# A hybrid decoder layer on one core: background work is offered a turn at each pair of main products instead of every six, with other constants in its estimate of time

## The chip, the cores and the metric

The kernel runs on one core of one Trainium2 chip. Its time is the device time of one execution in microseconds (us), given as the median of three runs. The engines of a core are named as in the profile: PE is TensorE's matrix products, PEld its weight loads, DVE is VectorE, ACT is ScalarE, POOL is GpSimd, SP is SyncE, which issues most DMAs here.

## The reference

One step of a decoder layer for two groups of requests that share all weights: a prompt of 512 new tokens, and eight sequences with one new token each. Width is 2048, everything is float32.

```
mod = silu(c) @ w_ada + b_ada              # 2048 x 12288, split into six parts
h = modulate(rmsnorm(x), sh1, sc1)
q, k, v, p_rwkv = split(h @ w_in)          # 4896 columns
att = sliding-window attention(q, k, v)    # 16 heads of 64, window 128, ALiBi, sinks
rw, S = RWKV-7 mixing(p_rwkv, S0)          # 16 heads of 64, a state recurrence over tokens
x = x + gt1 * (concat(att, rw) @ w_out)
h2 = modulate(rmsnorm(x), sh2, sc2)
x = x + gt2 * ((silu(gate) * up) @ w_ffn_out),   gate, up = split(h2 @ w_ffn_in)
y = rmsnorm(x)
```

Results are y for both groups, the new key and value windows, the new recurrent states and the last projection rows.

## The kernel before

**Main products.** Activations are kept transposed, 128 features by 2 x 260 columns (256 prompt tokens and four of the eight single tokens in each half). For precision each weight tile and each activation is split into a high and a low part of a reduced float32 type: `unit` (L81) loads 128 x 512 weights, ACT copies the high part (L88), DVE subtracts to get the low part (L91). `mm3` (L94) then issues three pairs of products for one block of 128 x 128 weights: high weights with the high activations, high with low, low with high, and in each pair one product for each half of the columns. These are the main products, `pm` in the profile for the input projection and the feed-forward part, `po` for the output projection, `pf` for the last projection. `main_tile` (L103) makes one tile of 128 output features from 16 blocks.

**Background work.** All that isn't such a product is written as generators, called jobs: the conditioning vectors (`ada_part` L272 in the startup, `ada_gen` L295 later, 256 steps of four small float32 products, each after a load of 256 KB), the RWKV mixing in eight pairs of heads (`rwkv_prep1`, `rwkv_prep2` and `rwkv_rest`, L530 to L790: preparation, a triangular solve in 31 steps on DVE, then a chain of 16 chunks with two steps each, where PE makes four records named `psc<-Z,L` or `psc<-Z,LS` and DVE and ACT copy them back), the attention in eight pairs of heads (`attn_pair` L857), the eight single tokens (`rwkv_sample` L1030, `attn_decode` L932), loads and splits (`cat_load` L1241), and the second norm (`norm_half` L1204). A job gives up its turn by `yield`.

**Who runs when.** `pump` (L123) is one turn. It advances the planner's clock of PE by the time that the main products since the last turn are thought to take, and then goes through the jobs: one that is due runs to its next `yield`, and its instructions come at this place of the program. When a job is next due is worked out by `spent` (L113): each instruction that a job issues through the `Paced` engines (L32 to L61) books a time on its engine's clock (a fixed part and a part per element) and moves `done_at`; what `done_at` is at the `yield` is when the job is due again. `main_tile`, `part_tile`, `wout_part` call `pump` once for each block, that is after six products, and `wout_half` (L1283) after three. A job that wants to wait yields more than once, or adds to `done_at`. `drain` (L137) and waiting loops call `pump` without main products.

The program order made in this way is not the last word: when the program is built, each engine's instructions are put in a list by a scheduler that prefers the earlier instruction and passes one whose inputs it doesn't think ready.

**Order of the kernel.** Startup (norm of x, the first two parts of the conditioning in stages, five first tiles); the RWKV phase with 39 tiles of the input projection in all, of which 12 are fillers (`filler` L437) that are taken when the next tile would have to wait for a buffer; the attention phase, whose main products are the output projection; the second norm, half by half, beside the last quarter of the output projection; and then the feed-forward part (`ffn_phase` L1307), in which no job is alive.

Of the kernel before, what the change touches and what calls it, by code (L numbers as in the profile page):

```python
# [8 lines left out]
F32R = mybir.dt.float32r  # L9
# [5 lines left out]
P = 128  # L15
# [16 lines left out]
class Paced:  # L32
# [5 lines left out]
    def __getattr__(self, name):  # L38
        f = getattr(self.eng, name)

        def call(out, *a, **kw):
            if name == "dma_start":
                self.kern.spent(self.eng, 1.0, 1.5)
            else:
                per = self.per
                if name == "matmul" and a[0].dtype == F32R:
                    per /= 4
                self.kern.spent(self.eng, self.base + per * math.prod(out.shape[1:]), 0.1)
            return f(out, *a, **kw)  # L49
        return call  # L50


class PacedCore:
    def __init__(self, kern):
        nc = kern.nc
        self.nc = nc
        self.tensor = Paced(kern, nc.tensor, 0.0017, 0.06)
        self.vector = Paced(kern, nc.vector, 0.0011, 0.08)
        self.scalar = Paced(kern, nc.scalar, 0.001, 0.2)
        self.gpsimd = Paced(kern, nc.gpsimd, 0.0023, 0.1)  # L60
        self.sync = Paced(kern, nc.sync, 0, 0)  # L61


class Kern:
    def __init__(self, tc, I, O, upto="all"):
        self.tc, self.nc, self.I, self.O, self.upto = tc, tc.nc, I, O, upto
        self.n = 0
        self.bg = []
        self.free, self.done_at = {}, 0.0
        self.px = PacedCore(self)  # L70
        self.nada = 0
        self.sample_done = self.kv_done = self.decode_done = False
        self.cat_out, self.cat_in = set(), 0
        self.psc = None
        self.squares = [None, None]
# [15 lines left out]
        nc.vector.tensor_tensor(wl[:, :n], raw[:, :n], wh[:, :n].bitcast(F32), ALU.subtract)  # L91
        return wh, wl

    def mm3(self, ps, m, wh, wl, aH, aL, k, first, last, halves=((0, 0), (1, 1))):  # L94
        nc = self.nc
        for i, (w, a) in enumerate(((wh, aH), (wh, aL), (wl, aH))):
            for h, bank in halves:
                nc.tensor.matmul(  # L98
                    ps[:m, bank, :HB], w, a[:, k, h, :],
                    start=first and i == 0, stop=last and i == 2, skip_group_check=True,  # L100
                )

    def main_tile(self, dram, aH, aL, ncol=128):  # L103
        ps = self.ps_m.tile([P, 2, 512], F32, tag="m", name=self.nm("pm"))
        for k in range(KD):
            if k % 4 == 0:
                wh, wl = self.unit(dram[:, k * ncol:(k + 4) * ncol])
            s = slice(k % 4 * ncol, (k % 4 + 1) * ncol)
            self.mm3(ps, ncol, wh[:, s], wl[:, s], aH, aL, k, k == 0, k == KD - 1)
            self.pump()  # L110
        return ps

    def spent(self, eng, us, more=0.0):  # L113
# [6 lines left out]
        self.free[self.nc.tensor] = self.free.get(self.nc.tensor, 0.0) + us  # L120
        return self.free[self.nc.tensor]

    def pump(self, us=0.62):  # L123

        self.now(us)
        for job in list(self.bg):
            if job[1] > self.now():
                continue
            self.done_at = self.now()
            if next(job[0], "end") == "end":  # L130
                self.bg.remove(job)
            job[1] = self.done_at

    def start(self, gen):
        self.bg.append([gen, 0.0])
# [136 lines left out]
    def ada_part(self, f):  # L272

        nc = self.nc
        ps = self.aux_c(f // 2 % 2)
        for kg in range(4):
            tag, n = (("RR", 2), ("L3", 3), ("As", 1), ("L3", 3), ("RR", 2), ("L3", 3))[self.nada % 6]
            self.nada += 1
            raw = self.rc.tile([P, 1024], F32, tag=tag, bufs=n, name=self.nm("araw"))
            nc.sync.dma_start(raw, self.I["w_ada1"][f // 2, kg])  # L280
            self.ada_mm(ps, raw, kg, 0, 256)
            self.spent(nc.tensor, 0.45)
            self.done_at += 0.7
            yield
        yield from self.ada_finish(f, 2, ps)
# [9 lines left out]
    def ada_gen(self):  # L295
        nc = self.px
        for c in (GT1, SH2, SC2, GT2):
            for q in range(4):
                ci = c // 4 + q
                ps = self.hold("ada")  # L300
                for k in range(KD):
                    raw = self.w.tile([P, 512], F32, tag="ar", bufs=3, name=self.nm("ar"))
                    nc.sync.dma_start(raw, self.I["w_ada2"][ci - 8, k])
                    for j in range(4):
                        self.nc.tensor.matmul(
                            ps[32 * j:32 * j + 32, 0:128], self.cT[:, k, :], raw[:, j * 128:(j + 1) * 128],
                            start=k == 0, stop=k == KD - 1, tile_position=(0, 32 * j), skip_group_check=True,
                        )
                    self.spent(self.nc.tensor, 0.3)
                    yield  # L310
                    yield
                res = self.w.tile([P, 512], F32, tag="ar", bufs=3, name=self.nm("adar"))[:, 0:128]
                nc.scalar.copy(res, ps[:, 0:128])
                yield
                p2 = self.aux("adT")
                nc.tensor.transpose(p2[:, 0:128], res, self.ident)
                nc.vector.tensor_tensor(
                    self.mod[:, 4 * ci:4 * ci + 4, :], p2[:, 0:128].rearrange("p (f t) -> p f t", f=4)[:, :, 0:9],
                    self.par[:, P_BA + 4 * ci:P_BA + 4 * ci + 4].unsqueeze(2).broadcast_to([P, 4, 9]), ALU.add)
# [86 lines left out]
    def part_tile(self, src, m, out, sout, k0, k1):  # L406
        nc = self.nc
        wh, wl = self.unit(src[:, k0 * m:k1 * m])
        ps = self.ps_m.tile([P, 2, 512], F32, tag="m", name=self.nm("pm"))
        for k in range(k0, k1):  # L410
            s = slice((k - k0) * m, (k - k0 + 1) * m)
            self.mm3(ps, m, wh[:, s], wl[:, s], self.hH, self.hL, k, k == k0, k == k1 - 1)
            self.pump()
        out = out.rearrange("p (h t) -> p h t", h=2)
        ps = ps[:m]
        sps = ps[:, :, HB - sout.shape[-1]:HB]
        if k0 == 0:
            nc.scalar.copy(out, ps[:, :, 0:256])
            nc.scalar.copy(sout, sps)
        else:  # L420
            nc.vector.tensor_tensor(out, out, ps[:, :, 0:256], ALU.add)
            nc.vector.tensor_tensor(sout, sout, sps, ALU.add)
# [107 lines left out]
    def rwkv_prep1(self, d):  # L530
# [13 lines left out]
        sq = t512("tF")  # L544
        k = self.shift_mix(8 + hp, sq)
        nc.scalar.activation(sq, k, AF.Square, scale=col(P_KK))
        for _ in range(3):
            yield
        pw = self.aux("pw")
        for i in range(2):  # L550
            nc.tensor.matmul(pw, lw[i][:, 0:128], self.LW, start=i == 0, stop=i == 1)
# [121 lines left out]
    def rwkv_rest(self, d):  # L673
# [103 lines left out]
        wh, wl = self.lora(hp, 384)  # L777
        nc.scalar.copy(wh[64:128, 128:256], wl[64:128, 128:256].bitcast(F32))
        yield
        for _ in range(3):  # L780
            yield
        pg = self.aux("pg")
        for i, (w, g) in enumerate(((wh, self.SG0[0]), (wh, self.SG0[1]), (wl, self.SG0[0]))):
            nc.tensor.matmul(pg, w[:, 0:128], g, start=i == 0, stop=False)
# [483 lines left out]
    def wout_part(self, k0, k1):  # L1268
        nc, I = self.nc, self.I
        while self.cat_in < k1 or (k0 == 8 and not self.decode_done):  # L1270
            self.pump()
        n = k1 - k0
        for o in range(KD):
            ps = self.ps_m.tile([P, 2, 512], F32, tag="m", name=self.nm("po"))
            for kk in range(n):
                if kk % 4 == 0:
                    wh, wl = self.unit(I["w_out"][o, :, (k0 + kk) * 128:(k0 + kk + 4) * 128])
                s = slice(kk % 4 * 128, (kk % 4 + 1) * 128)
                self.mm3(ps, P, wh[:, s], wl[:, s], *self.cat[0], k0 + kk, kk == 0, kk == n - 1)
                self.pump()  # L1280
            self.accumulate(o, ps, GT1)

    def wout_half(self, h, kept):  # L1283
# [3 lines left out]
        for o in range(0, KD, 2):  # L1287
            mt = lambda: self.ps_m.tile([P, 2, 512], F32, tag="m", name=self.nm("po"))
            ps = mt()
            for j in range(2):  # L1290
                if o + j not in kept:
                    pool = dict(pool=self.wk, bufs=6) if o in (2, 6, 10) else {}
                    u = self.unit(self.I["w_out"][o + j, :, 12 * 128:16 * 128], **pool)
                    if pool:
                        kept[o + j] = u
                wh, wl = kept.get(o + j, u)
                for kk in range(4):
                    s = slice(kk * 128, (kk + 1) * 128)
                    self.mm3(ps, P, wh[:, s], wl[:, s], *self.cat[1], kk, kk == 0, kk == 3, ((h, j),))
                    self.pump(0.4)  # L1300
                if o == KD - 2:
                    self.accumulate_half(o + j, 1, ps[:, j:j + 1], GT1, h)
                    ps = mt()
            if o < KD - 2:
                self.accumulate_half(o, 2, ps, GT1, h)
# [233 lines left out]
```

## Time and profile before

| what | value |
|---|---|
| median of three runs | 2763.02 us (2754.31 to 2765.76) |
| the profiled execution | 2761.62 us |
| its span, first to last instruction | 2759.8 us |
| busy: PE, PEld, DVE, ACT, POOL | 97%, 90%, 49%, 33%, 8% |
| mean granted clock of PE | 0.982 |
| main products: startup and input projection / output projection / feed-forward | 3744 / 1536 / 12672 |
| idle time of PE in the span | 80 us |

A row of the order of time is: start, duration, engine, line of the kernel, operation, output tile <- inputs, shape of the array's tile, shape of the data, number of records; in brackets idle time before it and the instruction that ended it. A float32 product shows as two records, one of the reduced type as one. L49 is the line of the helper that passes on the instructions of all jobs, so these are told apart by the names of their tiles. Products are pipelined: a row's duration is longer than its distance to the next, and the time that a group costs is read from the starts. A row of the waits is: engine, what waited, what it waited for, total us, times, longest.

### The profile page before, as it was taken

The page shows a single profiled execution, that of the slowest core. Times are in us where ns is not written, and L with a number is a line of the kernel's source. Part 1 is how long each engine was busy: PE and PEld are TensorE (multiplying, and loading weights), DVE is VectorE, ACT ScalarE, POOL GpSimd, SP SyncE. Part 2 cuts the span into 40 slices and gives each one's busy share as a digit, 9 for nine tenths or more (in the row PEclk, how much of TensorE's full clock was granted, in tenths as well). Part 3 has the DMA queues.
Part 4 walks back from the last instruction along what each step waited for, and adds up shares of the span by engine and source line. Part 5 has one row for each costly group of instructions (what it writes and reads, how often), then busy time and mean ns, then how long its engine had stood idle before and what let it go on. Part 6 is the DMA issues. An engine that isn't in the chain of part 4 may idle for free.

```text
span 2759.8 us, 58911 instructions
## 1 busy us (share of the span) xinstructions
PE 2679.3 (97%) x24461; PEld 2479.0 (90%) x24461; DVE 1356.5 (49%) x3266; ACT 923.4 (33%) x1816; POOL 223.6 (8%) x300
## 2 busy tenths in 40 slices
PE   7899999999999999989999999999999999999998
PEld 5577777887787898979999999999999999999997
DVE  2465677767755465682434343434343434343436
ACT  3133445455432344552222222222222222222225
POOL 1012122222111000130000000000000000000004
PEclk9899999999989999999999999999999999999999
DMA  8865554555556732322222222222222222222223
GB/s 296 308 200 149 153 152 141 161 150 151 175 163 206 255 133 100 113 80 92 91 93 90 93 92 93 92 92 93 92 93 92 92 93 92 93 92 93 90 96 110
DMA packets 189900, 354.25 MB, mean 128 GB/s; under 512 B 27665, under 2 KB 38849, under 8 KB 189345
## 3 DMA queue, kind: packets, MB, share of 16 engines
q1 hardware_dynamic: 185584, 339.30, 37.1%
q0 software_dynamic: 3408, 10.15, 1.2%
q8 instruction: 191, 3.13, 0.5%
q10 hardware_dynamic: 640, 1.05, 0.1%
q14 instruction: 77, 0.62, 0.1%
HBM read 332.86 MB, written 18.55 MB: 127 GB/s over the span
## 4 chain that ended last, share of the span: by engine, by line
PE 59%; DVE 2%; DMA 1%; ACT 1%; POOL 0%; issue 0%; DVEq 0%; SPq 0%; ACTq 0%; POOLq 0%
PE pm L98 36%; PE pf L98 18%; PE po L98 3%; PE pl L49 1%; PE pO L49 0%; PE pt L49 0%; PE psc L49 0%; DVE wl L91 0%; DVE x L1178 0%; DMA raw<-in_w_fi 0%; DVE h2L L49 0%; DVE u L49 0%; ACT h2H L49 0%; DMA raw<-in_w_out 0%; POOL u L49 0%
## 5 line engine op out<-in xcount | busy, mean ns | idle before, releaser
L88 ACT CAST wh<-raw 128x512 fp32r<-128x512 f32 (+2 forms) x751 | 460.9, 615 | 1266.8 <-PE pm L98 807.1
L91 DVE TENSOR_TENSOR wl<-raw,wh 128x512 fp32r<-128x512 f32 (+2 forms) x751 | 522.3, 697 | 690.2 <-ACT wh L88 688.8
L98 PE MATMUL pm<-h2H,wh 128*128 128x260 f32 x2816 | 571.2, 282 | 2.2 <-ACT wh L88 1.2
L98 PE MATMUL pm<-h2L,wh 128*128 128x260 f32 x2816 | 572.1, 283 | 0.7 <-DVE h2L L49 0.4
L98 PE MATMUL pm<-h2H,wl 128*128 128x260 f32 x2816 | 572.4, 283 | 0.0
L98 PEld LDWEIGHTS pm<-h2H,wh 128*128 128x128 f32 x2816 | 435.9, 188 | 2.9 <-ACT wh L88 1.3
L98 PEld LDWEIGHTS pm<-h2L,wh 128*128 128x128 f32 x2816 | 435.0, 188 | 1.7 <-DVE h2L L49 1.5
L98 PEld LDWEIGHTS pm<-h2H,wl 128*128 128x128 f32 x2816 | 436.3, 188 | 0.0
L98 PE MATMUL pm<-hH,wh 128*128 128x260 f32 (+1 forms) x1248 | 297.6, 318 | 2.8 <-ACT hH L143 1.6
L98 PE MATMUL pf<-gH,wh 128*128 128x260 f32 x1312 | 266.8, 283 | 0.0
L98 PE MATMUL pf<-gH,wl 128*128 128x260 f32 x1312 | 266.4, 282 | 0.0
L98 PE MATMUL pf<-gL,wh 128*128 128x260 f32 x1312 | 266.4, 282 | 0.0
L98 PE MATMUL pm<-hL,wh 128*128 128x260 f32 (+1 forms) x1248 | 264.7, 292 | 0.2 <-DVE hL L144 0.2
L98 PE MATMUL pm<-hH,wl 128*128 128x260 f32 (+1 forms) x1248 | 262.5, 291 | 0.0
L98 PEld LDWEIGHTS pm<-hH,wh 128*128 128x128 f32 (+1 forms) x1248 | 195.9, 192 | 51.8 <-issue 33.1
L1167 DVE SCALAR_TENSOR_TENSOR x<-pf,mod,x 128x512 f32<-128x512 f32 x160 | 120.1, 750 | 215.1 <-PE pf L98 215.1
L98 PEld LDWEIGHTS pf<-gH,wl 128*128 128x128 f32 x1312 | 203.4, 188 | 0.0
L98 PEld LDWEIGHTS pf<-gL,wh 128*128 128x128 f32 x1312 | 203.2, 188 | 0.0
L98 PEld LDWEIGHTS pf<-gH,wh 128*128 128x128 f32 x1312 | 203.2, 188 | 0.0
L98 PEld LDWEIGHTS pm<-hH,wl 128*128 128x128 f32 (+1 forms) x1248 | 197.6, 192 | 6.0 <-issue 1.8
L98 PEld LDWEIGHTS pm<-hL,wh 128*128 128x128 f32 (+1 forms) x1248 | 198.0, 192 | 5.4 <-issue 2.0
L1186 POOL TENSOR_TENSOR acc<-sqh 128x260 f32<-128x260 f32 x4 | 3.0, 742 | 1662.1 <-ACT sqh L1183 1471.3
(372 smaller groups left out, 3100.2 us busy)
## 6 DMA issues: line engine op xcount, KB each, us to landing
raw<-in_w_fi SPq DMA_DIRECT2D x352, 256.0 KB, 2.5
ar<-in_w_ada SPq DMA_DIRECT2D x256, 256.0 KB, 3.1
raw<-in_w_fo SPq DMA_DIRECT2D x176, 256.0 KB, 2.5
raw<-in_w_in SPq DMA_DIRECT2D x148, 256.0 KB, 3.6
araw<-in_w_ada SPq DMA_DIRECT2D x64, 512.0 KB, 6.0
raw<-in_w_out SPq DMA_DIRECT2D x74, 256.0 KB, 2.9
catl<-catd SPq DMA_DIRECT2D x16, 256.0 KB, 2.8
x<-in_x SPq DMA_DIRECT2D x4, 780.0 KB, 7.8
```

Of the source, the lines that this page charges most:

```text
L49: return f(out, *a, **kw)
L88: nc.scalar.copy(wh[:, :n], raw[:, :n])
L91: nc.vector.tensor_tensor(wl[:, :n], raw[:, :n], wh[:, :n].bitcast(F32), ALU.subtract)
L98: nc.tensor.matmul(ps[:m, bank, :HB], w, a[:, k, h, :], start=first and i == 0, stop=last and i == 2, skip_group_check=True,)
L1167: nc.vector.scalar_tensor_tensor(x[:, :, 0:256], ps[:, :, 0:256], self.mod[:, gt + o, 0:1], x[:, :, 0:256], ALU.mult, ALU.add)
L1186: nc.gpsimd.tensor_tensor(acc, sq[:, 0], sq[:, 1], ALU.add)
```

## The change

`mm3` gets an argument `pump` and offers a turn after each pair of products; `main_tile`, `part_tile` and `wout_part` use it and no longer pump once for six. The time that a turn adds to the planner's clock goes from 0.62 for six products to 0.243 for two. The estimate of an instruction's time changes for PE: another slope and fixed part, 0.12 for a transpose, 0.05 for a product on a part of the array, a quarter for the reduced type as before. A turn in which a job used PE now adds 0.2 (`switched`). Jobs that waited by yielding several times now yield once and add a time to `done_at`: 1.6 for each step of `ada_gen`, 2.2 in `rwkv_prep1` and `rwkv_rest`. Turns without main products add 0.73 in place of 0.62, and the half-product loop 0.37 in place of 0.4. No instruction is added or removed.

```diff
@@ Paced.call
-                per = self.per
-                if name == "matmul" and a[0].dtype == F32R:
-                    per /= 4
-                self.kern.spent(self.eng, self.base + per * math.prod(out.shape[1:]), 0.1)
+                us = self.base + self.per * math.prod(out.shape[1:])
+                if name == "transpose":
+                    us = 0.12
+                elif name == "matmul":
+                    us = 0.05 if kw.get("tile_position") else us / 4 if a[0].dtype == F32R else us
+                if self.eng is self.kern.nc.tensor:
+                    self.kern.switched = True
+                self.kern.spent(self.eng, us, 0.1)
@@ PacedCore
-        self.tensor = Paced(kern, nc.tensor, 0.0017, 0.06)
+        self.tensor = Paced(kern, nc.tensor, 0.002, 0.03)
@@ mm3
-    def mm3(self, ps, m, wh, wl, aH, aL, k, first, last, halves=((0, 0), (1, 1))):
+    def mm3(self, ps, m, wh, wl, aH, aL, k, first, last, halves=((0, 0), (1, 1)), pump=0):
...
+            if pump:
+                self.pump(pump)
@@ main_tile (part_tile and wout_part alike)
-            self.mm3(ps, ncol, wh[:, s], wl[:, s], aH, aL, k, k == 0, k == KD - 1)
-            self.pump()
+            self.mm3(ps, ncol, wh[:, s], wl[:, s], aH, aL, k, k == 0, k == KD - 1, pump=0.243)
@@ pump
-    def pump(self, us=0.62):
+    def pump(self, us=0.73):
...
+        if self.switched:
+            self.switched = False
+            self.now(0.2)
@@ ada_part
-            self.spent(nc.tensor, 0.45)
+            self.spent(nc.tensor, 0.3)
+            self.switched = True
@@ ada_gen
-                    self.spent(self.nc.tensor, 0.3)
-                    yield
+                    self.spent(self.nc.tensor, 0.15)
+                    self.switched = True
+                    self.done_at += 1.6
                     yield
@@ rwkv_prep1, rwkv_rest
-        for _ in range(3):
-            yield
+        self.done_at += 2.2
+        yield
@@ wout_half
-                    self.pump(0.4)
+                    self.pump(0.37)
```

More of the change, by code (lines that the diff above doesn't have):

```diff
@@ L68, in __init__ @@
         self.bg = []
-        self.free, self.done_at = {}, 0.0
+        self.free, self.done_at, self.switched = {}, 0.0, False
         self.px = PacedCore(self)
@@ L411, in part_tile @@
             s = slice((k - k0) * m, (k - k0 + 1) * m)
-            self.mm3(ps, m, wh[:, s], wl[:, s], self.hH, self.hL, k, k == k0, k == k1 - 1)
-            self.pump()
+            self.mm3(ps, m, wh[:, s], wl[:, s], self.hH, self.hL, k, k == k0, k == k1 - 1, pump=0.243)
         out = out.rearrange("p (h t) -> p h t", h=2)
@@ L779, in rwkv_rest @@
         yield
-        for _ in range(3):
-            yield
+        self.done_at += 2.2
+        yield
         pg = self.aux("pg")
@@ L1278, in wout_part @@
                 s = slice(kk % 4 * 128, (kk % 4 + 1) * 128)
-                self.mm3(ps, P, wh[:, s], wl[:, s], *self.cat[0], k0 + kk, kk == 0, kk == n - 1)
-                self.pump()
+                self.mm3(ps, P, wh[:, s], wl[:, s], *self.cat[0], k0 + kk, kk == 0, kk == n - 1, pump=0.243)
             self.accumulate(o, ps, GT1)
```

## The prediction

> **What bounds the kernel now.** I read the page first, then busy time by stretch, then the groups of TensorE instructions by line, the waits, and last the order of time on TensorE (PE) inside the stretch that the change reaches.
>
> ```profile
> PE 2679.3 (97%) x24461; PEld 2479.0 (90%) x24461; DVE 1356.5 (49%) x3266; ACT 923.4 (33%) x1816; POOL 223.6 (8%) x300
> ```
>
> PE is busy for 97% of the span. The table of stretches (columns: length, busy time of PE, PEld, DVE, ACT, POOL, granted clock, DMA share, GB/s) tells which part of that can move:
>
> ```profile
> 0.00:150.00 150.00, 120.27 (x996) 83.34 (x996) 57.86 (x163) 38.48 (x79) 12.16 (x29) 0.90 0.81 295
> 150.00:935.00 785.00, 763.26 (x8495) 623.75 (x8492) 522.25 (x1361) 343.26 (x731) 148.15 (x198) 0.97 0.55 165
> 935.00:1150.00 215.00, 212.29 (x1882) 193.54 (x1881) 117.66 (x403) 91.03 (x249) 4.00 (x8) 0.98 0.40 138
> 1150.00:1241.00 91.00, 78.72 (x582) 74.59 (x580) 76.63 (x173) 51.27 (x98) 31.17 (x36) 0.96 0.30 102
> 1241.00:2760.00 1519.00, 1504.79 (x12518) 1503.74 (x12516) 582.07 (x1170) 399.33 (x661) 28.11 (x30) 1.00 0.27 93
> ```
>
> The last 1519 us are the feed-forward part; no background job is alive there. The first 150 us run at 295 GB/s with the DMA engines 81% busy: their conditioning weights set the pace, so turns there cost nothing and gain nothing. What the change reaches is 150 to 1150 us, and in it PE idles only 785.0 - 763.3 = 21.7 us and 215.0 - 212.3 = 2.7 us. So this stretch is a sum of PE work, and a gain has to come out of 24.4 us of idle time or out of the work itself.
>
> ```profile
> PE psc L49 <- ACT Z L49: 6.3, 14, 1.2
> PE pu L49 <- DVE L L49: 4.8, 1, 4.8
> PE ada L305 <- DMA ar<-in_w_ada: 3.6, 3, 1.5
> ```
>
> These are the three longest waits of PE between 150 and 1150 us (total, times, longest). The first is the background chain of the state recurrence: 14 of its steps came to PE too early and held the queue for 6.3/14 = 0.45 us each.
>
> **Term 1: visits of PE to the background.** The groups of 150 to 935 us give the number of steps (a float32 product shows as two records):
>
> ```profile
> L98 PE MATMUL pm<-hH,wh 128*128 128x260 f32 (+1 forms) x1128 | 268.6, 317 | 0.0
> ...
> L305 PE MATMUL ada<-ar,cT 128*32 128x128 f32 x2048 | 112.3, 289 | 3.9 <-DMA ar<-in_w_ada 3.6
> L49 PE MATMUL psc<-Z,LS 128*64 128x64 f32 x512 | 44.0, 247 | 5.1 <-ACT Z L49 4.7
> L49 PE MATMUL psc<-Z,L 128*32 128x64 f32 x512 | 38.3, 228 | 2.1 <-ACT Z L49 1.6
> ```
>
> The first row is one of three alike: 3 x 1128 = 3384 main products. 2048 records at 8 a step are 256 conditioning steps (ada); 512 at 4 are 128 chain steps of each kind, 256 in all. I counted in the order of time how these stand between the main products. From the first of the next two rows to the last, PE leaves the main products 403 times; 133 of the visits hold both an ada and a chain step, and of 145 other steps (transposes, preparation, solve, output) 100 share a visit with one of these two.
>
> ```profile
> 150.61 0.61 PE L49 MATMUL adT<-cst,adar 128*128 128x9 f32 x4 [0.55 <-ACT adar L49]
> ...
> 926.19 0.32 PE L49 MATMUL adT<-cst,adar 128*128 128x128 f32 x1
> ```
>
> What sharing saves is read from three visits (start, duration). An ada step alone:
>
> ```profile
> 421.88 0.34 PE L49 MATMUL psc<-Z,LS 128*64 128x64 f32 x4 [0.15 <-ACT Z L49]
> 422.14 0.39 PE L98 MATMUL pm<-hL,wh 128*128 128x260 f32 x1
> 422.37 0.40 PE L98 MATMUL pm<-hH,wl 128*128 128x260 f32 x2
> 422.70 0.42 PE L305 MATMUL ada<-ar,cT 128*32 128x128 f32 x8
> 423.05 0.51 PE L98 MATMUL pm<-hH,wh 128*128 128x260 f32 x2
> 423.39 0.41 PE L98 MATMUL pm<-hL,wh 128*128 128x260 f32 x2
> ```
>
> Two undisturbed pairs follow each other by 0.24 us (405.33 to 405.57 us in the third visit below); the 0.10 us more from 423.05 to 423.39 are the way back to them. From 422.37 to 423.39 are 1.02 us, less two pairs 0.48: 0.54 us. A chain step alone:
>
> ```profile
> 428.04 0.40 PE L98 MATMUL pm<-hL,wh 128*128 128x260 f32 x2
> 428.37 0.31 PE L49 MATMUL psc<-Z,L 128*32 128x64 f32 x4
> 428.61 0.50 PE L98 MATMUL pm<-hH,wl 128*128 128x260 f32 x2
> 428.95 0.40 PE L98 MATMUL pm<-hH,wh 128*128 128x260 f32 x2
> ```
>
> 0.91 - 0.48 = 0.43 us. Both in one visit:
>
> ```profile
> 404.19 0.40 PE L98 MATMUL pm<-hH,wl 128*128 128x260 f32 x2
> 404.52 0.42 PE L305 MATMUL ada<-ar,cT 128*32 128x128 f32 x8
> 404.78 0.28 PE L49 MATMUL psc<-Z,L 128*32 128x64 f32 x4
> 404.99 0.51 PE L98 MATMUL pm<-hH,wh 128*128 128x260 f32 x2
> 405.33 0.40 PE L98 MATMUL pm<-hL,wh 128*128 128x260 f32 x2
> 405.57 0.40 PE L98 MATMUL pm<-hH,wl 128*128 128x260 f32 x2
> ```
>
> 1.14 - 0.48 = 0.66 us, against 0.54 + 0.43 = 0.97: a shared visit saves 0.31 us. For the other chain step (another tile shape, 128*64) I take less; between 0.31 and the 0.2 that the change's own constant gives a switch I use 0.25 us. A visit of untiled transposes is cheaper:
>
> ```profile
> 956.35 0.40 PE L98 MATMUL po<-cH,wl 128*128 128x260 f32 x2
> 956.59 0.38 PE L49 MATMUL ptx<-cst,vf 128*128 128x128 f32 x2
> 956.72 0.49 PE L98 MATMUL po<-cH,wh 128*128 128x260 f32 x2
> 957.05 0.41 PE L98 MATMUL po<-cL,wh 128*128 128x260 f32 x2
> ```
>
> 0.70 - 0.48 = 0.22 us for two: hardly any switch. For the "other" steps the price of a visit of their own lies between 0 and 0.31; I take 0.20, as many of them are tiled.
>
> Now the planner's clock, from its constants. Before: a chain step books 0.44 us on PE and is due 1.35 us after its start; with turns 0.62 apart it comes at the second turn (0.44 + 2 x 0.62 = 1.68), and ada comes at each second turn by its two yields. Both have a period of two turns, so they meet in one of two: 133 of 256 is that. After: a chain step books 0.20, is due after 1.11, the switch adds 0.20, turns are 0.243 apart: 0.40 + 3 x 0.243 = 1.13, the third turn. Ada is due 1.75 after its start and comes after 0.35 + 6 x 0.243 = 1.81, less what chain steps add. If the phase is free, ada meets the chain's turn in one of three: 85 of 256. Lost: 133 - 85 = 48, at 0.25 us 12.0 us. The other steps shared a visit in 100 of 145, as 403 visits on about 3384/6 = 564 turns make two turns in three taken; with 1692 turns and some 450 visits only one in four is, but long steps let others fall due, so I take 55. Lost 45 at 0.20: 9.0 us. In 935 to 1150 us only 6 steps share a visit (77 steps, 71 visits, same count): 6 x 0.2 = 1.2 us. Bounds of the term: 0 if all sharing is kept, 133 x 0.31 + 100 x 0.2 + 1 = 62 us if none is.
>
> This is where a rule speaks against the change: the Trainium skill (TensorEngine Tiling (Array Packing), Key Properties) says that a change of the tiling mode, not of the tile, drains the TensorE. The rows agree in kind: the tiled visits pay, the transposes do not. By that rule the untiled half of the 45 would pay nothing and the tiled half 0.31, 7 us in place of 9, and the sum would be 2783.
>
> **Term 2: waits.** Finer turns let a step start nearer to its due time; what goes is a part of the waits outside the chain (21.7 - 6.3 = 15.4 us; I take 6). What comes: chain steps six products apart, 0.72 + 0.43 = 1.15 us, while the step at 421.88 still waited. Now 14 of 256 wait; twice that is +6.3. I take the two as equal, 0 us, with bounds -18 and +32 (a third of the chain steps at 0.45 us is 38, less 6).
>
> **Terms at nothing.** Ada runs at each 10 products, not 12, so its loads are issued more densely on SP's queue, ahead of some weight loads:
>
> ```profile
> ar<-in_w_ada SPq DMA_DIRECT2D x256, 256.0 KB, 3.1
> ```
>
> They land in 3.1 us, three buffers hold 5 us at 1.8 us a step, and the DMA engines are at 55%: hidden; without that cover the 3.6 us of waits would double. The steps of 2.2 us that replace three yields only shift one wait for a load. The half-product loop (0.40 to 0.37) serves a norm whose steps are due at once, so its order stays. Drain and idle turns (0.62 to 0.73) only count time. DVE works 522 of 785 us, so a background done 15% sooner takes it to about 78%: still not the bound. Finishing sooner gains nothing, as main products are left to the end (PE is 212.3 of 215 us busy after it).
>
> Sum: 12.0 + 9.0 + 1.2 + 0 = 22 us on the profiled execution's 2761.62 (its span and 1.8 us around it): 2784. That execution lies 1.4 us under the median of 2763.02; against the median: **2785 us**.
>
> **Rivals.** (a) Faster: the finer turn takes the waits away and sharing is kept. For it: PE's order is not the planner's alone; at 422.14 a single product follows a chain step, so an instruction that is not due is already passed by single products, which could push chain steps against ada again. Against it: the chain's waits lie just where steps come early. All but 6 us of the 21.7 gone: 2763 - 16 = 2747. It decides if under some 30 shared visits are lost. (b) No change: because of that same passing, the real order hardly depends on the turn, or terms 1 and 2 cancel: 2763. (c) Slower still: the chain, now planned at its shortest latency, holds PE again and again: 22 + 32, 2817. It decides from about one chain step in three waiting. The 14 waits of 256 speak against it, the 0.45 us each for it.
>
> **How the numbers follow.** My forecast 0.36 (its own range 2772 to 2800), (c) 0.14, (b) 0.26, (a) 0.24. About 0.5% (14 us) is what a measurement of this kernel can tell from no change. Slower holds the forecast and (c), 0.50; faster 0.22, as (a) lies just beyond the bound; same 0.28, the rest. The range runs from (a) to just past (c), 2745 to 2820.
>
> **What would show it.** Right: between the same two instructions more than 403 visits (450 to 520), fewer with ada and chain together, chain steps nearer 1.3 us apart, the feed-forward part unchanged at 1519 us. Wrong: about 400 visits or fewer, or PE idle in that stretch far under 20 us with the stretch shorter; and if visits rise but the stretch does not, the price of a visit was wrong.

## The result and the profile after

| | before | after |
|---|---|---|
| median, 4 runs each | 2758.66 us (2752.75 to 2765.76) | 2884.77 us (2880.79 to 2896.81) |
| ratio, 95% interval | | 1.046 (1.0425 to 1.0495) |
| span of the profiled execution | 2759.8 us | 2884.0 us |
| granted clock of PE | 0.982 | 0.974 |

The change costs 126 us. Forecast was a loss of 22. The page after, its span and its first row of busy time:

```profile
span 2884.0 us, 58956 instructions
...
PE 2786.8 (97%) x24461; PEld 2531.0 (88%) x24461; DVE 1346.9 (47%) x3266; ACT 928.9 (32%) x1820; POOL 210.1 (7%) x300
```

The same 24461 records of products are done, PE is busy for the same 97%, and yet its busy time grew by 107.5 us (2679.3 before). The share of busy time says nothing here: the same products take more time. The table of stretches, cut where the background starts (first `ada`), where the input projection ends and where the feed-forward part runs freely; of after:

```profile
160.00:1046.00 886.00, 851.98 (x8465) 668.61 (x8464) 508.50 (x1352) 344.39 (x726) 134.01 (x196) 0.95 0.49 144
1046.00:1338.00 292.00, 276.71 (x2298) 253.55 (x2296) 173.45 (x534) 128.69 (x318) 31.38 (x40) 0.95 0.37 127
...
1365.00:2884.00 1519.00, 1504.83 (x12516) 1503.58 (x12515) 581.81 (x1169) 399.25 (x660) 28.11 (x30) 1.00 0.27 93
```

and of before, for the first two of them:

```profile
154.00:933.00 779.00, 757.86 (x8461) 619.26 (x8461) 518.37 (x1352) 338.75 (x722) 147.12 (x196) 0.98 0.55 165
933.00:1215.00 282.00, 269.68 (x2303) 248.16 (x2302) 173.73 (x532) 128.10 (x316) 31.29 (x40) 0.97 0.38 131
```

From `ada` to the last input product is 107 us more, with four more records; the output projection and the second norm are 10 us more, the startup 6 us; the feed-forward part is the same: PE is busy for 1504.83 of its 1519 us, and for 1504.79 before. Idle time in the first stretch is 34.0 us after and 21.1 before, so 13 of the 107 us are idle time. The longest waits of after there (total, times, longest):

```profile
PE psc L53 <- ACT Z L53: 9.6, 12, 4.8
PE ada L314 <- DMA ar<-in_w_ada: 7.8, 14, 1.5
PE pu L53 <- DVE TT L53: 7.0, 4, 2.6
```

Before they were 6.3, 3.6 and 4.8: little. The other 94 us are busy time. The groups by tile show where; three of after, then two of before (records | busy, mean ns | idle):

```profile
L314 PE MATMUL ada<-ar,cT 128*32 128x128 f32 x2048 | 129.0, 288 | 8.7 <-DMA ar<-in_w_ada 7.8 <-ACT wh L92 0.5
...
L53 PE MATMUL pY<-Z,RR 128*32 128x64 f32 x512 | 51.5, 229 | 1.6 <-DVE Z L53 1.5
...
L53 PE MATMUL pA<-tC,KB 64*64 64x32 f32 x512 | 41.1, 248 | 2.6 <-DVE L L53 1.4 <-DVE mod L53 1.2
```

```profile
L49 PE MATMUL pA<-tC,KB 64*64 64x32 f32 x512 | 20.9, 220 | 1.3 <-DVE mod L49 1.2
...
L49 PE MATMUL pY<-Z,RR 128*32 128x64 f32 x512 | 9.3, 222 | 0.0
```

`pY`, the output of the recurrence, is the same 512 records at nearly the same mean, 222 and 229 ns, and takes 51.5 us in place of 9.3. Records overlap when they follow each other; busy time counts the overlap once. So the records have been pulled apart. The order of time of after shows how:

```profile
322.91 0.40 PE L102 MATMUL pm<-hL,wh 128*128 128x260 f32 x2
323.25 0.30 PE L53 MATMUL pY<-Z,RR 128*32 128x64 f32 x2
323.48 0.51 PE L102 MATMUL pm<-hH,wl 128*128 128x260 f32 x2
323.82 0.28 PE L102 MATMUL pm<-hH,wh 128*128 128x260 f32 x1
324.03 0.34 PE L53 MATMUL psc<-Z,LS 128*64 128x64 f32 x4
324.30 0.30 PE L53 MATMUL pY<-Z,RR 128*32 128x64 f32 x2
324.52 0.39 PE L102 MATMUL pm<-hH,wh 128*128 128x260 f32 x1
```

As the kernel is written, the 64 records of a head pair come after its last chain step. Here two of them go each time a chunk of `Z` is there, in the middle of the chain, some on a visit of their own. This is how I read it: the order in which the jobs were asked has run far ahead of the chain, the chain steps wait for their inputs, and the scheduler fills in later instructions that can go. In the program as it is built, `pY` stands in 163 separate places, and in 8 before.

`pA` (the scores, in `rwkv_prep2`) shows the second kind of damage. Before, one that stands whole, and one in two halves:

```profile
358.94 2.06 PE L49 MATMUL pA<-tC,KB 64*64 64x32 f32 x64
360.93 0.51 PE L98 MATMUL pm<-hH,wh 128*128 128x260 f32 x2
```

```profile
204.56 2.02 PE L49 MATMUL pA<-tC,KB 64*64 64x32 f32 x32
206.51 0.50 PE L98 MATMUL pm<-hH,wh 128*128 128x260 f32 x2
206.94 2.05 PE L49 MATMUL pA<-tC,KB 64*64 64x32 f32 x32
208.92 0.51 PE L98 MATMUL pm<-hL,wh 128*128 128x260 f32 x2
```

64 records take 1.99 us to the next row, and 32 (one half) take 1.95 and 1.98. The two heads of a pair sit on different quadrants of the array and run side by side; a half alone runs alone. The Trainium skill (TensorEngine Tiling (Array Packing), Key Properties) says that different tiles load weights and multiply in parallel; these rows agree. Before, two of eight pairs were in halves; after, seven, and some with the clock down:

```profile
631.49 0.51 PE L102 MATMUL pm<-hH,wh 128*128 128x260 f32 x2 [1.62 <-ACT wh L92]
631.84 0.40 PE L102 MATMUL pm<-hL,wh 128*128 128x260 f32 x2
633.52 2.04 PE L53 MATMUL pu<-TT,L 128*128 128x128 f32 x8 [1.29 <-DVE TT L53]
...
635.50 3.62 PE L53 MATMUL pA<-tC,KB 64*64 64x32 f32 x32
639.05 0.65 PE L314 MATMUL ada<-ar,cT 128*32 128x128 f32 x8
639.63 0.58 PE L102 MATMUL pm<-hH,wl 128*128 128x260 f32 x1
640.15 3.62 PE L53 MATMUL pA<-tC,KB 64*64 64x32 f32 x32
```

From 632.48 us the granted clock is at 0.50 for 17 us, and a half of `pA` takes 3.6 us in place of 2.

To add this up I took, in the order of time from the first `ada` to the first `po` of each kernel, the distance from each row's start to the next row's start, and gave it to the row's tile. Before that is 779.3 us, after 885.6.

| us, start to start | before | after | more |
|---|---|---|---|
| main products | 510.7 | 544.6 | 33.9 |
| `pY` | 8.6 | 34.3 | 25.7 |
| `ada` | 90.5 | 110.2 | 19.7 |
| `pA` | 21.4 | 40.0 | 18.6 |
| all others | 148.1 | 156.5 | 8.4 |

The main products' share is ways above all: what the last row before a visit and the first behind one take above 0.12 us a product, waits apart, was 85.0 us for 402 visits and is 111.2 for 514, 0.21 and 0.22 us a visit, 26.2 us more. Some 7 us are waits.

The clock is in all these rows and is not taken apart from them. One minus the granted clock, summed over the same stretch, is 41.0 us after and 19.4 before. By that sum, as an estimate, it can account for at most some 22 of the 106 us: 11 lie in `pA`, 6 in the main products.

### The profile page after: what moved, and what is told of

The parts are those of the page before. It is cut to its first block, busy times and chain, and to the rows that moved or that the text cites. A ratio compares the mean times of both kernels' runs of the same rounds, so it can differ in the third digit from the quotient of the medians.

```text
span 2884.0 us, 58956 instructions
## 1 busy us (share of the span) xinstructions
PE 2786.8 (97%) x24461; PEld 2531.0 (88%) x24461; DVE 1346.9 (47%) x3266; ACT 928.9 (32%) x1820; POOL 210.1 (7%) x300
## 4 chain that ended last, share of the span: by engine, by line
PE 60%; DVE 3%; DMA 2%; ACT 1%; issue 0%; POOL 0%; DVEq 0%; ACTq 0%; POOLq 0%; SPq 0%
PE pm L102 35%; PE pf L102 17%; PE po L102 5%; PE psc L53 1%; PE pl L53 1%; PE pO L53 1%; DVE wl L95 1%; DMA raw<-in_w_out 0%; PE pt L53 0%; DMA catl<-catd 0%; DVE x L1187 0%; DMA raw<-in_w_fo 0%; ACT wh L92 0%; DMA raw<-in_w_fi 0%; DVE h2L L53 0%
## 5 line engine op out<-in xcount | busy, mean ns | idle before, releaser
L102 PE MATMUL pm<-hH,wl 128*128 128x260 f32 (+1 forms) x1248 | 295.2, 306 | 6.7 <-DVE wl L95 6.7
L102 PE MATMUL pm<-hH,wh 128*128 128x260 f32 (+1 forms) x1248 | 291.6, 305 | 6.4 <-ACT wh L92 4.7
L102 PE MATMUL pm<-hL,wh 128*128 128x260 f32 (+1 forms) x1248 | 286.3, 303 | 0.2 <-DVE hL L152 0.2
L314 PE MATMUL ada<-ar,cT 128*32 128x128 f32 x2048 | 129.0, 288 | 8.7 <-DMA ar<-in_w_ada 7.8
```

Source lines behind the costliest of these rows:

```text
L102: nc.tensor.matmul(ps[:m, bank, :HB], w, a[:, k, h, :], start=first and i == 0, stop=last and i == 2, skip_group_check=True,)
L314: self.nc.tensor.matmul(ps[32 * j:32 * j + 32, 0:128], self.cT[:, k, :], raw[:, j * 128:(j + 1) * 128], start=k == 0, stop=k == KD - 1, ti ...
```

## The experiments

The plan is the order in which the turns put the jobs' steps between the main products. The theory: the finer turn, whatever the constants, lets the plan run ahead of the recurrence, because a job takes one step at a turn, and a turn of six products was what held it back. Ahead of the chain, `pY` and `pA` come apart, and each part costs. The rivals: the new constants do it; it is the number of visits alone, at the prediction's price, as fewer of them are shared by two jobs; the chain's latency sets the time. "Places" are uninterrupted runs of a tile in the order of PE; from the same order come the visits. All ratios are to the kernel before, run beside each experiment on the same chip, where its median was 2758.7 to 2761.4 us; so a few us between two experiments mean little.

**1. A turn for six products, the new constants** (`main_tile`; `part_tile` and `wout_part` alike)

```diff
-            self.mm3(ps, ncol, wh[:, s], wl[:, s], aH, aL, k, k == 0, k == KD - 1, pump=0.243)
+            self.mm3(ps, ncol, wh[:, s], wl[:, s], aH, aL, k, k == 0, k == KD - 1)
+            self.pump(0.729)
```

> After, with a turn once for six main products again (0.729 a turn), every other constant as in after. Theory: the finer turn, not the constants, makes the plan run ahead of the recurrence. In this kernel's order of instructions the output products pY stand at 12 places (163 after, 8 before), pA at 9 (15, 10) and PE leaves the main products 439 times (514, 402). So only the visits cost: 37 more than before at 0.2 to 0.3 us, 2759 + 7 to 11, about 2768 us (2760 to 2780). Rival, the constants do it (a chain step due after 1.1 us instead of 1.35, ada after 1.75): the loss stays for the most part, over 2840 us.

Measured: 2777.88 us, ratio 1.0059 (1.0035 to 1.0083). 107 of the 126 us are gone with the turn; the constants are left with some 16.

**2. The fine turn, the old constants**

```diff
-            self.mm3(ps, ncol, wh[:, s], wl[:, s], aH, aL, k, k == 0, k == KD - 1)
-            self.pump()
+            self.mm3(ps, ncol, wh[:, s], wl[:, s], aH, aL, k, k == 0, k == KD - 1, pump=0.207)
```

> Before, with a turn at each pair of products (0.207, a third of 0.62) and all the old constants. Theory of the finer turn: pY stands at 74 places, pA at 13, and 467 visits: 65 x 0.25 = 16 us for visits, 66 of 155 more places of pY = 0.43 x 26 = 11, 3 more halves of pA at 2 us and the low clock behind them 10 to 15: about 2800 us (2785 to 2825). Rival, the constants: 2759 to 2770 us, as before.

Measured: 2887.82 us, 1.0466 (1.0419 to 1.0514): the whole loss of the change, without its constants. With run 1 this settles the turn as the cause. That the two losses are equal is chance, as they are made up otherwise, and my sum for this kernel was 88 us short: among other things it left out how the plan ends. Its stretches, up to the last input product, then to the first output product:

```profile
154.00:997.00 843.00, 791.15 (x8275) 633.02 (x8275) 487.52 (x1298) 325.70 (x681) 138.71 (x193) 0.95 0.51 149
997.00:1051.00 54.00, 33.14 (x244) 19.45 (x244) 20.80 (x71) 12.86 (x42) 7.43 (x12) 0.54 0.58 198
```

The first stretch is 64 us longer than before (106 after the change), and 54 us lie between the last input product and the first output product. Conditioning is done at 611 us (925 before), and the chain of the last pair stands alone at the end, with no main product left to go beside it:

```profile
1017.56 0.42 PE L49 MATMUL pY<-Z,RR 128*32 128x64 f32 x2 [0.40 <-DVE Z L49]
1017.91 0.48 PE L49 MATMUL psc<-Z,LS 128*64 128x64 f32 x4
1018.32 0.42 PE L49 MATMUL pY<-Z,RR 128*32 128x64 f32 x2
1019.19 0.43 PE L49 MATMUL psc<-Z,L 128*32 128x64 f32 x4 [0.44 <-ACT Z L49]
```

For most of these 54 us PE has hardly anything but this, 1.2 us a step at a granted clock of 0.54. In this kernel's plan the chains of the first three pairs cover 122 to 130 main products each, and the next four 396 to 594 (282 to 336 in these seven before): it runs ahead at first and is late at its end. After the change itself there is no such gap (the last input product at 1045.56 us, the first output product at 1045.68).

**3. `pY` held together.** In `rwkv_rest`, ahead of the products:

```diff
+        for r, eng in ((0, nc.vector.tensor_copy), (64, nc.scalar.copy)):
+            eng(pY[r:r + 64].rearrange("p (q n) -> p q n", q=4), L3[0:64, 1, 0, :].unsqueeze(1).broadcast_to([64, 4, 128]))
```

> After, with the output products pY of a head pair kept in one burst: two copies of the final state into all of pY, on DVE and ACT, come ahead of them, so none can start before the last chain step. 8 places in place of 163; pA stays at 15 places, visits 471 in place of 514. Theory, pieces of pY cost by themselves (34.3 us after, 8.6 before, from start to start) and by the ways back to the main products (43 x 0.1): 2885 - 26 - 4 = 2855 us. Rival, the number of visits alone, at the 0.25 us of the prediction: 43 x 0.25 = 11, 2874 us. Rival, the latency of the chain sets the time: no gain, 2885 us or more, as two copies are added at its end.

Measured: 2866.32 us, 1.0381 (1.0348 to 1.0414), 18.5 us less. Its group:

```profile
L53 PE MATMUL pY<-Z,RR 128*32 128x64 f32 x512 | 9.3, 222 | 0.0
```

The work is back to 9.3 us, as before; of the 30 us that I counted 18 to 19 arrive. In this kernel's profile `ada` waits 15.8 us for its loads and the chain 17.1, where it was 7.8 and 9.6, and one minus the granted clock sums to 51.2 us of the stretch, where it was 41.0. So part of the gain goes into waits and into the clock.

**4. `pA` in one buffer.** The two heads write to the lower and the upper half of the partitions of one PSUM buffer (the masking on DVE behind it follows, and is left out here):

```diff
-        pA = [self.aux("pA"), self.aux("pA")]
+        pA = self.aux("pA")
...
-                nc.tensor.matmul(pA[e][64:128, c * 32:(c + 1) * 32], KBc(ri, c), rt[ri, c * 32:(c + 1) * 32],
-                                 start=True, stop=True, skip_group_check=True, tile_position=(64 * e, 64))
+                nc.tensor.matmul(pA[ri, c * 32:(c + 1) * 32], KBc(ri, c), rt[ri, c * 32:(c + 1) * 32],
+                                 start=True, stop=True, skip_group_check=True, tile_position=(64 * e, 64 * e))
```

> After, with the two halves of pA in one buffer of PSUM, one in the lower and one in the upper partitions, instead of two buffers, so that its 64 records can't be split into two halves of 32. Theory: a half costs as much as the whole (1.98 us from start to start), and two halves behind each other, some 4 us of it, let the granted clock fall to 0.5 to 0.8 for the 10 to 20 us behind. pA 40.0 us to 16 to 21 and some 32 us x clock deficit behind the halves mostly gone: -20 - 20, about 2845 us (2835 to 2855). If the clock falls for another reason: pA alone, 2865 us. If only visits count (476 for 514): 2875 us.

Measured: 2853.92 us, 1.034 (1.0303 to 1.0378), 31 us less.

```profile
L53 PE MATMUL pA<-tC,KB 64*64 64x32 f32 x512 | 18.9, 229 | 1.7 <-DVE L L53 1.3 <-DVE mod L53 0.4
```

22 us of the 31 are in this row (41.1 after). The clock is better as well: over slices of 10 us from 160 to 940 us, what the granted clock lacks of 1 sums to 37.7 us after, 13.7 here and 17.1 before.

**5. Both.** The edits of 3 and 4.

> After, with both edits of the last two runs: pY in one burst (18.5 us less by itself) and pA in one buffer (31 us less by itself). Theory, two separate losses: 2885 - 50 = 2835 us; PE leaves the main products 448 times (402 before, 514 after), so 46 visits at about 0.21 us of ways in and out, 10 us, are left of the loss by visits, and the rest of the 2835 - 2759 = 76 us is waits, conditioning steps cut in pieces and what lies behind the input projection. Rival, both edits win by the same thing (fewer visits, or one buffer of PSUM being free): about 2850 us, hardly better than the better one.

Measured: 2832.19 us, 1.0262 (1.0241 to 1.0282): 52.6 us less, where the two by themselves give 18.5 + 30.9 = 49.4. So they are two separate losses. The clock does not go with whole `pA` alone: here, with `pA` whole too, the sum of run 4 is 27.3 us. 72 us over before are left. The waits of PE in the stretch to 992 us, and the stretch:

```profile
PE ada L314 <- DMA ar<-in_w_ada: 15.0, 26, 1.5
PE pu L53 <- DVE TT L53: 12.3, 6, 3.4
PE psc L53 <- ACT Z L53: 11.0, 15, 3.5
```

```profile
157.00:992.00 835.00, 788.48 (x8462) 622.44 (x8461) 512.87 (x1361) 348.78 (x735) 136.44 (x196) 0.97 0.53 154
```

Its idle time is 835.0 - 788.5 = 46.5 us, 25 more than before; 31 us are busy time (46 more visits, conditioning cut in 289 places where before had 258); the rest, some 15 us, lies ahead of it and behind it.

**6. The fine turn with a cap.** A job that ran is not offered a turn before the third turn after (`self.turn`, which `pump` counts up at its start, is left out here):

```diff
         for job in list(self.bg):
-            if job[1] > self.now():
+            if job[1] > self.now() or us < 0.3 and self.turn < job[2]:
                 continue
+            job[2] = self.turn + 3
```

> After, with the turn at each pair of products kept and all its constants, but a job that has run is not offered a turn again before the third turn after (six main products). Theory: the due times hardly bind, as the planner's clock runs on by 0.6 us for each main product; what held the jobs back in the kernel before was that a job got at most one step for six products, so this cap alone brings the time back. pY at 10 places, pA at 9, 469 visits: 67 more than before at 0.21 to 0.25 us, 2761 + 14 to 17, about 2778 us (2768 to 2795). Rival, the fine turn itself (jobs that no longer meet in one visit, other order of the loads): 2840 us or more.

Measured: 2781.69 us, 1.0083 (1.006 to 1.0105). 103 of 126 us are back, with the turn at each pair and all the constants of the change:

```profile
162.00:947.00 785.00, 763.70 (x8466) 614.97 (x8465) 514.25 (x1357) 336.79 (x725) 138.97 (x196) 0.99 0.57 164
```

785 us against 779 before, although PE leaves the main products 469 times, 67 more often. So these 103 us are not the price of asking at each pair, but of jobs that take their steps faster than one for six products. The number of visits does not set the time either: runs 5, 11 and 12 have 448, 453 and 448 visits, of which `ada` and the chain share 64, 80 and 66, and take 2832, 2778 and 2849 us.

**7. `pY` in pieces, in the kernel before.** The two products of a chunk go one by one with the chain steps of the next chunk:

```diff
+        pY = self.aux("pY")
         for c in range(16):
             ps = self.aux_c(hp % 2)
+            if c:
+                piece(c - 1, 0)
...
+            if c:
+                piece(c - 1, 1)
             dst = Z[0:64, c + 1] if c < 15 else SF
```

> Before, with the output products of a chunk issued with the chain steps of the next chunk, so that pY lies in 246 pieces and holds one of the two spare PSUM buffers through the chain, as it does after the change. The planner and its turns are those of before. Theory, pieces cost by themselves: pY from 8.6 to some 35 us (+26), 58 more visits at 0.21 us (+12), pA at 16 places in place of 10 (+12): about 2810 us (2790 to 2830). Rival, pieces only show that the plan runs ahead and cost nothing much: 2761 to 2775 us.

Measured: 2829.96 us, 1.0257 (1.0234 to 1.028): 69 us lost without any change of the planner.

```profile
L49 PE MATMUL pY<-Z,RR 128*32 128x64 f32 x512 | 72.5, 228 | 0.0
...
L49 PE MATMUL pA<-tC,KB 64*64 64x32 f32 x512 | 36.9, 232 | 0.9 <-DVE RR L49 0.7
```

`pA` is in halves in all eight pairs. It needs two of two spare PSUM buffers, and `pY` holds one of them through the chain. So pieces of `pY` tear `pA` apart too. In run 3, however, `pY` was whole and `pA` still in 15 places: there other work must have held a buffer, which no run traced.

**8. `pA` in one buffer, in the kernel before.** The edit of 4.

> Before, with pA in one buffer. Before, two of the eight head pairs had pA in two halves (at 204 and at 268 us), at 1.98 us each, with a granted clock of 0.84 and 0.66 in the ten us behind. Theory: 2 x 1.98 us less, and up to 5 us of low clock: 2761 - 4 to 9, about 2755 us. Rival, the split is hidden: 2761 us.

Measured: 2754.09 us, 0.9975 (0.9962 to 0.9987). 6.5 us under the kernel before, a small gain whose interval leaves out 1; no other edit here gains on it. The clock of 0.66 that I expected behind the halves at 268 us lies ahead of them: it is at 0.50 for 6.8 us from 261.03 us, and at 1 behind them.

**9, 10. Fewer visits.** Two conditioning steps are done at one visit (two loads, eight products, and twice the yields; in 10 three yields), 9 in the kernel of 8, 10 in that of 1 with `pA` in one buffer.

```diff
-                for k in range(KD):
+                for k2 in range(0, KD, 2):
...
-                    self.spent(self.nc.tensor, 0.3)
-                    yield
-                    yield
+                    self.spent(self.nc.tensor, 0.6)
+                    for _ in range(4):
+                        yield
```

> Before with pA in one buffer (2754 us), and the conditioning two steps at a visit, with four yields instead of two behind them. PE leaves the main products 352 times, 398 without it. Theory, a visit costs some 0.21 us of ways in and out (85.0 us of the stretch before, over 402 visits) and a further 0.1 for a tiled step: 46 visits are 10 to 14 us, 2740 to 2744 us. Against it: two loads of 256 KB must be there at once in three buffers, waits for them were 3.6 us in all and could triple; and the last chain ends behind the last product of the input projection in the plan, by up to 43 turns more without main products: up to 25 us lost. Theory that these eat it: 2754 to 2770 us.

Measured: 2769.37 us, 1.0039 (1.0025 to 1.0054). Its stretch of input products is 759 us, 11 less than in run 8, and then PE waits for the last chain:

```profile
913.40:936.00 22.60, 7.45 (x104) 5.40 (x103) 7.27 (x25) 6.25 (x15) 6.83 (x11) 0.72 0.91 308
```

> After with a turn for six products (2778 us), pA in one buffer, and two conditioning steps at a visit. 357 visits, 439 with neither, and here the last chain ends with 600 main products to spare in the plan. Theory, visits at 0.21 to 0.3 us: 82 of them are 17 to 25 us: 2753 to 2761 us. If a visit is free as long as the step is done anyway: 2775 to 2778 us.

Measured: 2773.06 us, 1.0046 (1.0033 to 1.006), against 1.0059 in run 1. Here there is no gap at the end, and 82 fewer visits, together with `pA` in one buffer, bring next to nothing. The ways fell from 90.6 to 76.3 us, but the waits grew; of run 10, then of run 1:

```profile
PE psc L53 <- ACT Z L53: 24.2, 40, 1.8
PE ada L318 <- DMA ar<-in_w_ada: 15.8, 15, 1.6
```

```profile
PE ada L315 <- DMA ar<-in_w_ada: 6.3, 5, 1.6
...
PE psc L53 <- ACT Z L53: 3.2, 10, 0.5
```

Where other work no longer fills the chain's latency, PE waits for the chain instead.

**11. The cap with the old constants** (run 2 with the cap of 6 and `pA` in one buffer).

> Before with pA in one buffer (2754 us), all old constants, a turn at each pair of products (0.207) and a job not again before the third turn after its last. Without the cap and the one buffer this turn gave 2888 us. Theory, the cap of one step for six products is all that the coarse turn did: pY at 13 places, 453 visits, 55 more than 398, at 0.13 to 0.25 us: 2761 to 2768 us. Rival, the fine turn costs by itself: 2800 us or more. Another, with the plan held the finer place of a step wins back waits: under 2750 us.

Measured: 2778.14 us, 1.0068 (1.0052 to 1.0083). The cap and the one buffer take 110 us off run 2, but a finer place for each step does not win: this is 24 us over run 8, and more than I expected. Its stretch is 791.7 us, 21.7 more than in run 8, for 55 more visits: 0.39 us each, nearer to the price of an unshared tiled step than to the ways alone.

**12. The chain's due time alone**

```diff
-            self.done_at += 0.2
+            self.done_at += 1.1
```

(both of the chain's steps)

> After, with the chain's own pace put back by its due time alone: 1.1 us in place of 0.2 is added behind each step. As the program is written, the 32 steps of a head pair then cover 242 to 280 main products in the first six pairs (122 to 138 after, 282 to 312 before). Theory, each job's pace matters, and preparation, solve and conditioning still run ahead (a solve covers 120 to 160 main products, 204 to 306 before): the plan is ahead of the chain before it starts, so pY stays at 54 places, pA at 12, 448 visits: from 2885 us 109 of 155 pieces' places less (17), 3 halves of pA (8), 66 visits at 0.21 (14), about 2846 us (2830 to 2860). Rival, the chain's due time is the one wrong constant: 2780 us.

Measured: 2848.64 us, 1.0321 (1.0289 to 1.0353). 36 of the 126 us come back, so the chain's due time by itself is not the cause. In this plan the chains cover 242 to 280 main products in the first six pairs (282 to 312 before), but a triangular solve still covers 124 to 170 in the first seven, where it was 210 to 312 before: the other jobs' pace counts as well.

## Why the prediction was wrong

**The side was right, the size was not: 22 us for 126.** What the forecast counted, the ways in and out of visits, came to 26 us. `pY` and `pA`, for which it has no term, are 44 of the 106 us in the stretch.

**The step that failed** is in term 1, "the planner's clock, from its constants": "0.40 + 3 x 0.243 = 1.13, the third turn". I let the clock advance by the turns and the job's own cost alone. As the programs are written, the 32 steps of a chain cover 122 to 138 main products in the first seven pairs after, that is four products a step, not six, and 282 to 336 before, nine or ten, not twelve. The reason is in `spent` (L113), which I had described and not applied: an instruction that depends on an earlier one of its job sets its engine's clock forward to `done_at`. Waiting of any job that uses PE thus moves the clock of all. From the start of a pair's chain to its end the clock moves 74 to 84 us for those 122 to 138 products, 0.6 us a product, where a product takes 0.12; some three fifths of that are such jumps, under a third is what the turns add. Due times of 1.1 or 1.75 us are then over in a turn or two. What held the jobs back before was that one gets a single step at a turn. Runs 1, 2 and 6 show this: with a turn or a cap of six products 198 to 254 products for the chain's 32 steps (first seven pairs) and 2778 to 2782 us; with neither, 2885 and 2888 us.

**What followed from it** is the second failed step, which the prediction does not even state: that a step of the background costs the same wherever it comes. The sum has a price for visits and for waits, and none for the steps themselves. `pY` (25.7 us from start to start) and `pA` (18.6) were no term at all. Runs 3, 4, 5 and 7 show that they cost by themselves: 18.5 and 31 us, 52.6 both, and 69 us in the kernel before with `pY` issued in pieces.

**Term 1 as a count** held: 514 visits (450 to 520 forecast), 64 with both ada and chain (85 forecast, 133 before), and 112 more visits where 93 shared ones were to be lost in this stretch. The ways are 26 us, against 22. But the price is not a law: 67 more visits cost 5 us of the stretch in run 6, 55 cost 21.7 in run 11, and 82 fewer brought 3 us of the stretch in run 10 (783.7 to 781.0). The clock is part of these differences: what it lacks sums to 19.4 us before and to 8.5 in run 6, so 5 us is too little for those 67.

**Term 2**, waits, at 0 with bounds of -18 and +32: idle time in the stretch grew by 13 us. Within the bounds. Rival (c) forecast a slower case by chain steps that hold PE; the chain held it 12 times, not 85, so it was not that. "Chain steps nearer 1.3 us apart" was wrong: between 318 and 328 us they are 1.5 to 2.1 us apart.

**Terms at nothing.** "Finishing sooner gains nothing" held for conditioning (done at 849 us for 925) but missed the other end: a job that is done sooner leaves less to cover the last chain. After the change, that cost nothing; in runs 2 and 9 it left stretches of 54 and 23 us in which PE is busy for 33 and 7. The startup cost 6 us and the output projection 10, where I had 0 and 1.2; in run 1 they are 4 and 7, so these come from the constants for the most part, and no run took them apart further.

**Left open**: why the clock fell in some places with halves of `pA` and not in others (in run 7, in halves throughout, behind three of the eight pairs the slices of 10 us were above 0.97), and what the 72 us of run 5 are, more than half of the loss: its profile divides them into 25 us of waits, 31 of busy time and some 15 outside the stretch, but no experiment took them apart.

## What to carry to other kernels

A queue of background jobs is held back by whatever binds first, and that may be how often it is asked, not the due times that are written down. Before the turn is made finer, count how many units of foreground work each job's step covers in the program, and compare it with how far apart the chip runs those steps; where the program is faster, the scheduler may tear later work apart to fill in. A finer turn needs a cap of its own, and here it was no gain even with one: runs 6 and 11 are 21 and 18 us over the kernel before.

## What the runs showed of the hardware that I had not expected

64 records of small products in two quadrants of the array take 1.99 us and 32 in one quadrant 1.98. Here products that alternate between two tiles were worth keeping together, and an output in one PSUM buffer did that (run 8: 6.5 us for one edit).

The 512 records of `pY` cost 8.6 us in eight bursts before, 1.08 us each, and 34.3 us in 163 places after.

The granted clock fell to 0.50 at 632.48 us, after a gap of 1.62 us and within one of 1.29: a row of half of `pA` shows 3.62 us there, and 2.05 where the clock is at 1. The Trainium skill (TensorE: Matmul & The Clock Gate, Part 1: The HAM clock gate) puts the step to half rate after an idle window of about 3.4 us; the factor of 1.8 is near to that, but no single gap in these rows is that long. At 284.32, 721.22 and 905.54 us the clock fell to 0.50 too, with no gap over 0.15 us in the 3.4 us before, in which 32 to 46 records of `pA` lie; so in this trace the clock also falls where PE was not idle, and that is not explained here.
